# A hybrid SSD, attention and convolution layer: another order of pairs in the input projection, and attention's loads on another queue

## The chip, the cores and the metric

The kernel runs on one core of a Trainium2 chip. A core has a matrix engine (TensorE; PE in the profile, with PEld for its weight loads), three engines for element-wise work (VectorE or DVE, ScalarE or ACT, GpSimd or POOL) and SyncE (SP), which here only issues DMAs. The engines run side by side; each takes its own instructions strictly in order and waits on semaphores for the others. A DMA is issued by an instruction in an engine's queue (SPq, POOLq in the profile) and lands later. The metric is device time in microseconds for one execution; lower is better.

## The reference

One inference step of a one-layer streaming encoder for 1024 prompt positions and 64 positions of a running stream (1088 columns in all). Cut to what matters:

```python
xn = _rmsnorm(x, p['norm_mix_w'])
proj = xn @ p['w_in']
z, xbc, dt_raw, q, k, v, gate_ssm, gate_att = jnp.split(proj, ...)

xbc_c, conv_new = _causal_dwconv(conv_past, xbc, ...)     # 4 taps
xbc_c = jax.nn.silu(xbc_c)                                # then the SSD scan gives y_ssm
y_ssm = _rmsnorm(y_ssm * jax.nn.silu(z))                  # in groups

q = _partial_rope(_rmsnorm(q, p['q_norm_w']), q_pos)
k = _partial_rope(_rmsnorm(k, p['k_norm_w']), q_pos)
s = q @ k.T * ATT_HEAD_DIM ** -0.5                        # two components per head
a = softmax(s)[:, 0] - lam * softmax(s)[:, 1]
o = _rmsnorm(a @ v_all) * (1.0 - lambda_init)

mix = sigmoid(gate_ssm) * (y_ssm @ w_branch_ssm) + sigmoid(gate_att) * (o @ w_branch_attn)
x = x + mix @ w_out
x = x + (silu(conv(rmsnorm(x) @ w_up_a)) * (rmsnorm(x) @ w_up_b)) @ w_down
```

## The kernel before

Every large product is made of three matmuls on split operands: `hi` is the operand rounded to float32r (a cast on ACT, L404), `lo` is the rest (a subtraction on DVE, L405), and the sum is hi x hi + hi x lo + lo x hi. The function `split` (L403) makes both halves.

**Stages in order.** Values and time steps (to about 117 us); the pair stage (117 to 724 us), which projects q, k, z and the convolution's channels; attention over 8 heads (742 to 1120 us), with the gates and the last z tiles as filler between its units; the SSD scan; the branches; the FFN.

**The pair stage.** A pair is two 128-row weight blocks, multiplied by a scheme of 7 block products where a plain one needs 8. Product p takes one combination of the weights (`left[n][p]`, made by `left_parts`, L470 on) and one of the inputs (`parts[PARTS[p], s]`, with `PARTS` = b11, t2, b21, t3, t1, t4, b22). Each product runs in two halves s of 272 columns, with 12 matmuls per half (L553). `in_pair` (L540) is a generator: each `send((p, s))` issues the matmuls of one half and the evacuation behind it. p=0 and p=2 are evacuated by ACT (`u1`, L622; `pre`, L633), the others by DVE with an addition (L624, L626, L635). A pair that has its four quadrants calls `done` (L591): a z pair gets a SiLU on ACT; a q or k pair gets squares (ACT L610, L613; DVE L614) that are summed for its norm; a convolution pair gets, for each of four quadrants, one ACT pass (L581), three DVE passes (L583) and a SiLU (L584). q, k and z pairs are called light here. `INPUT` (L74) gives the order of the 26 pairs: four q, four k, three z, and then three times four convolution pairs and a z pair.

**Where the input parts come from.** b11, b21 and t2 are made in place. t3, t1, t4 and b22 are written to scratch memory p_sc by `rooted` and come back through `load_part` (L534): two loads on SP and a split of each. b12 takes a place that is only free at the stage's end.

**Work beside.** `beside` is a chain of small generators, stepped once in every four sends (L818): `steps` (the time steps' softplus, decays), `cached_keys` (splits of the cached keys), and from pair 3 on `finishing("q")` and `finishing("k")`: for each kind three norm roots (`rstd_of`: ACT Ln L241, Exp L242), twelve row parts (load, scale by DVE L735, split, two stores) and four rotated parts (DVE L749 to L756). Its tiles are called x. The scheduler fixes the order on each engine when the kernel is built; `tc.issue_after(i)` keeps what it encloses behind instruction i.

**Attention.** Per head, `head_tiles` (L883) loads 33 pieces through `load`, which is `nc.sync.dma_start`, SP's queue: q and the halves kh and kl of k for two components c and two column sides x (22 loads; side 0 holds columns 0 to 511), v_t in two loads, and ch_t, cl_t, cv_t of the cache in nine. The side tiles have three buffers, so a component of the next head waits for one of the last. `attend` does one unit: the scores of a block of 128 queries (L959, L960), exponentials (ACT L973), and two units later transposes (L988) and the product with the values (L1008). `ATT_ORDER` = (3, 7, 0, 6, 1, 5, 2, 4, 8): unit i below 8 needs keys up to 128(i+1), unit 8 is the running stream with the cache. Filler comes from `project` (L162), whose weights are loaded by `weights` (L144: load L147 on SP, cast on ACT L148, subtraction on DVE L149). Six such groups (144 matmuls) run between the last pair and the end of the first scores.

Of the kernel before, what the change touches and what calls it, by code (L numbers as in the profile page):

```python
# [9 lines left out]
F32 = mybir.dt.float32  # L10
# [35 lines left out]
B_Q, B_K, B_V, B_Z, B_X, B_G = 0, 8, 16, 20, 36, 60  # L46
WMAX = 4 * (256 + 16)

ATT_ORDER = (3, 7, 0, 6, 1, 5, 2, 4, 8)
BG = 8  # L50
TURNS = ((0, 1), (2,), (3,), (4,), (5,), (6, 7))
# [19 lines left out]


ORDER = (("g", (15, 14)), ("z", range(4 * ZS, 16)), ("g", range(13, 7, -1)), ("g", range(7, 1, -1)))
INPUT = ([(k, i) for k in "qk" for i in range(4)]  # L74
         + [("z", i) for i in range(ZS)] + [x for i in range(ZS) for x in (*(("c", 4 * i + j) for j in range(4)), ("z", ZS + i))])

O_MIX, O_FFN, O_CW, O_CB, O_SN, O_D = 0, 8, 16, 112, 136, 152
O_QN, O_KN, O_FW, O_FB, O_CS = 168, 176, 184, 250, 272
# [5 lines left out]
def hybrid_layer(ctx: ExitStack, tc: tile.TileContext, xT, xt, prm, cst, rope, wvd, win, wbs, wba, wout, wup, wdn,  # L84
# [318 lines left out]
    def split(hi, lo, src):  # L403
        S.copy(hi, src)  # L404
        V.tensor_tensor(out=lo, in0=src, in1=hi, op=ALU.subtract)  # L405

    def cols(s):
        return slice(O2[s], O2[s] + W2[s])
# [108 lines left out]
            left.setdefault(f, {})[x[0]] = x[1]  # L517

    FIRST_BLOCK = dict(q=B_Q, k=B_K, c=B_X, z=B_Z)
    squares, begun_squares = {}, set()  # L520
    seen = {}

# [11 lines left out]
    def load_part(n, at=None):  # L534
        for s in range(2):
            hi, lo = parts[n, s] = units_of(n, s, at)
            load(out=lo.bitcast(F32), in_=p_sc[n].rearrange("(k p) t -> p k t", p=P)[:, :, cols(s)])
            split(hi, lo, lo.bitcast(F32))

    def in_pair(n):  # L540

# [76 lines left out]
        for _ in range(14):  # L618
            p, s = at
            us = cols(s)  # L620
            if p == 0:
                S.copy(u1[:, us], pile("a", p, s, True))  # L622
            elif p == 1:
                seen["read"] = V.tensor_tensor(out=u2[:, us], in0=pile("b", p, s, True), in1=u1[:, us], op=ALU.add)  # L624
            elif p == 3:
                seen["read"] = V.tensor_tensor(out=u1[:, us], in0=pile("b", p, s, False), in1=u1[:, us], op=ALU.add)  # L626
            else:
                r, c, key, start, u = {2: (0, 0, "a", False, None), 4: (1, 1, "c", True, u1), 5: (1, 0, "d", True, u1),
                                       6: (0, 1, "c", False, u2)}[p]
                ps = pile(key, p, s, start)  # L630
                for dst, x in to(r, c, s):
                    if u is None:
                        S.copy(dst, ps[:, x])  # L633
                    else:
                        seen["read"] = V.tensor_tensor(out=dst, in0=ps[:, x], in1=u[:, us][:, x], op=ALU.add)  # L635
                if s == 1:
                    done(r, c)
            at = yield
# [147 lines left out]

    four = row("ss", "st")
    early = [plain_left(0), plain_left(1)]
    for n in ("t3", "t1", "t4", "b22"):
        load_part(n)  # L790
    left = {}
    coming = in_parts(0, early[0])
    for _ in range(7):
# [3 lines left out]
    rest = [(p, s) for p in (1, 3, 4, 5, 6) for s in range(2)]  # L797
    pairs = [begun_in(0), begun_in(1)]
    left[1] = {0: [t[:, :512] for t in early[1]], 2: [t[:, 512:] for t in early[1]]}
    for i in range(2):  # L800
        for at in both:
            pairs[i].send(at)
    for p, s in rest:
        pairs[0].send((p, s))
        if s == 1:
            more_left(1)
    while len(left[1]) < 7:
        more_left(1)
    beside = chain(steps(), cached_keys())
    for n in range(1, len(INPUT)):  # L810
        coming = in_parts(n + 1) if n + 1 < len(INPUT) else iter(())
        u = pairs[1] if n == 1 else begun_in(n)
        for at, (p, s) in enumerate(rest if n == 1 else [(p, s) for p in range(7) for s in range(2)]):
            u.send((p, s))
            if s == 1:
                more_left(n + 1)
            if at % 4 == 0:
                next(beside, None)  # L818
            if n + 1 == len(INPUT) and (p, s) == (1, 1):
                load_part("b12")  # L820
        while n + 1 < len(INPUT) and len(left[n + 1]) < 7:
            more_left(n + 1)
        del left[n]
        if n == 3:
            beside = chain(beside, finishing("q"), finishing("k"))
    run(beside)
    plain = [k_rows(parts, c, s) for c in range(2) for s in range(2)]
# [53 lines left out]
    with (tc.tile_pool(name="ak", bufs=1) as ak, tc.tile_pool(name="at", bufs=1) as at,  # L881
          tc.tile_pool(name="psc", bufs=1, space=PSUM) as psc, tc.tile_pool(name="psa", bufs=1, space=PSUM) as pa):
        def head_tiles(h):  # L883
            def fetch(name, n, b, parts):
                t = ak.tile([P, n], R32, name=name, tag=name, bufs=b)
                for lo, src in parts:
                    load(out=t[lo : lo + src.shape[0]].bitcast(F32), in_=src)
                return t

            by_head = lambda d: [d.rearrange("(x h) t -> h x t", h=16)[2 * h + c] for c in range(2)]  # L890
# [17 lines left out]
            cv_t = ak.tile([P, 4, P], F32, name="cv_t", tag="cv_t", bufs=2)  # L908

            def values_of():  # L910
                load(out=v_t[:, :8], in_=v[0:TP, P * h : P * (h + 1)].rearrange("(a p) e -> p a e", p=P))
                load(out=v_t[:TS, 8], in_=v[TP:T, P * h : P * (h + 1)])

            def cached():
                past(0, ch_t, "ch_t")
                past(1, cl_t, "cl_t")
                load(out=cv_t, in_=cv[:, P * h : P * (h + 1)].rearrange("(a p) e -> p a e", p=P))

            if h == 0:
                for x in range(2):  # L920
# [154 lines left out]
        for h in range(8):  # L1075
# [7 lines left out]
            s0 = at.tile([P, 9], F32, name="s0", tag="s0", bufs=2)  # L1083
            V.memset(ssq, 1.0)
            V.memset(s0, 1.0)
            for x, i in enumerate(ATT_ORDER):
                unit = attend(h, i, tiles, o_t, ssq, s0)
                next(unit)
                next(ended, None)
                done = None  # L1090
                if i == ATT_ORDER[-1]:
                    done = lambda h=h, o=o_t, q=ssq, s=s0: head_out(h, o, q, s)
                waiting.append((unit, done))
                settle(DEEP, ATT_STEPS)
# [708 lines left out]
```

## Time and profile before

| | |
|---|---|
| Median of three runs | 2511.06 us (2508.02 to 2512.3) |
| The profiled execution, its own time | 2511.3 us |
| Span of its instructions | 2509.5 us |
| Matmul clock granted, mean | 0.991 |
| DMA, share of 16 engines | 52.5% SP's queue, 3.4% POOL's |

The page gives busy time per engine and what ended the idle time ahead of a group of instructions. A view by stretches gives busy time for each engine between two moments. The timeline lists instructions by start, with a bracket that says how long the engine had been idle and which instruction released it. L numbers are lines of this kernel; a matmul's duration overlaps with the next one's, so a group's share is better read from busy time than from the mean. DMA rows give the count, the size of each and the median time from issue to landing.

### The profile page before, as it was taken

The page shows a single profiled execution, that of the slowest core. Times are in us where ns is not written, and L with a number is a line of the kernel's source. Part 1 is how long each engine was busy: PE and PEld are TensorE (multiplying, and loading weights), DVE is VectorE, ACT ScalarE, POOL GpSimd, SP SyncE. Part 2 cuts the span into 40 slices and gives each one's busy share as a digit, 9 for nine tenths or more (in the row PEclk, how much of TensorE's full clock was granted, in tenths as well). Part 3 has the DMA queues.
Part 4 walks back from the last instruction along what each step waited for, and adds up shares of the span by engine and source line. Part 5 has one row for each costly group of instructions (what it writes and reads, how often), then busy time and mean ns, then how long its engine had stood idle before and what let it go on. Part 6 is the DMA issues. An engine that isn't in the chain of part 4 may idle for free.

```text
span 2509.5 us, 48443 instructions
## 1 busy us (share of the span) xinstructions
PE 2390.5 (95%) x18504; PEld 2302.9 (92%) x18504; DVE 1782.3 (71%) x3063; ACT 1231.0 (49%) x2615; POOL 720.0 (29%) x702
## 2 busy tenths in 40 slices
PE   8999999989989899999999999999999999999999
PEld 8999998888988788889888899999999999999999
DVE  4595778889957776762778765665977777776763
ACT  7344446435435566554767664434443333343441
POOL 0012213344400000000534342002264554544433
PEclk9999999999999999999999999999999999999999
DMA  7845463754265565525598973766123335258874
GB/s 252 271 154 190 176 225 109 247 186 145 100 185 167 158 184 154 161 90 199 192 333 274 309 253 128 216 183 208 56 88 144 114 113 185 78 208 224 221 204 83
DMA packets 282442, 449.72 MB, mean 179 GB/s; under 512 B 34969, under 2 KB 185634, under 8 KB 282210
## 3 DMA queue, kind: packets, MB, share of 16 engines
q1 hardware_dynamic: 275010, 433.54, 52.5%
q0 software_dynamic: 7200, 13.09, 3.4%
q8 instruction: 145, 2.38, 0.4%
q14 instruction: 87, 0.71, 0.1%
HBM read 294.03 MB, written 152.50 MB: 178 GB/s over the span
## 4 chain that ended last, share of the span: by engine, by line
PE 62%; DVE 13%; DMA 11%; ACT 6%; issue 4%; POOL 2%; SPq 1%; DVEq 0%; POOLq 0%; ACTq 0%
PE mx L553 9%; PE mx L1464 8%; PE mx L1622 5%; PE mm L155 5%; PE mm L157 5%; PE mm L156 5%; PE mm L553 4%; PE mm L1464 3%; PE mx L155 2%; PE po L1008 2%; PE mm L1622 2%; PE mx L157 2%; PE mx L156 2%; DMA ht<-h_sc 2%; DVE cc L583 1%
## 5 line engine op out<-in xcount | busy, mean ns | idle before, releaser
L155 PE MATMUL mm<-b,w_hi 128*128 128x272 f32 x1152 | 342.9, 298 | 4.8 <-ACT w_hi L148 2.9
L157 PE MATMUL mm<-b,w_lo 128*128 128x272 f32 x1152 | 339.5, 295 | 2.1 <-DVE w_lo L149 2.1
L156 PE MATMUL mm<-b,w_hi 128*128 128x272 f32 x1152 | 340.1, 295 | 0.0
L155 PEld LDWEIGHTS mm<-b,w_hi 128*128 128x128 f32 x1152 | 220.3, 191 | 9.8 <-issue 3.7
L157 PEld LDWEIGHTS mm<-b,w_lo 128*128 128x128 f32 x1152 | 219.8, 191 | 5.8 <-DVE w_lo L149 3.7
L156 PEld LDWEIGHTS mm<-b,w_hi 128*128 128x128 f32 x1152 | 220.3, 191 | 3.0 <-issue 2.1
L1143 POOL TENSOR_SCALAR_AFFINE_SELECT bc<-bc 128x1024 f32<-128x1024 f32 (+1 forms) x36 | 43.0, 1196 | 581.6 <-DMA start<-in_st_dram 471.7
L480 POOL TENSOR_TENSOR ws<-w_f 128x512 f32<-128x512 f32 (+1 forms) x56 | 79.5, 1420 | 416.4 <-DVE ss L614 159.9
L405 DVE TENSOR_TENSOR wh<-w_f,wh 128x512 fp32r<-128x512 f32 (+1 forms) x174 | 163.3, 939 | 46.5 <-ACT wh L404 46.1
L404 ACT CAST w_hi<-ws 128x512 fp32r<-128x512 f32 (+1 forms) x120 | 73.3, 611 | 186.0 <-PE mx L1464 84.6
L1464 PE MATMUL mx<-n,wh 128*128 128x272 f32 x1128 | 150.1, 288 | 1.9 <-ACT wh L404 1.3
L1464 PE MATMUL mx<-m,w_hi 128*128 128x272 f32 x752 | 146.0, 291 | 3.1 <-DVE hb L1500 2.9
L1464 PEld LDWEIGHTS mx<-n,wh 128*128 128x128 f32 x1128 | 144.5, 188 | 2.5 <-ACT wh L404 1.6
L973 ACT ACTIVATE p_t<-sc,mx 128x512 f32<-128x512 f32 (+5 forms) x144 | 106.1, 739 | 66.3 <-DVE mx L964 22.8
L583 DVE SCALAR_TENSOR_TENSOR cc<-pre,par,cc 128x544 f32<-128x544 f32 (+1 forms) x144 | 131.9, 937 | 0.3 <-ACT cc L581 0.2
L404 ACT CAST wh<-w_f 128x512 fp32r<-128x512 f32 (+1 forms) x174 | 106.5, 615 | 50.1 <-issue 15.3
L553 PE MATMUL mx<-t,wh 128*128 128x272 f32 x840 | 116.0, 291 | 11.6 <-DVE u L624 10.3
L1464 PEld LDWEIGHTS mx<-m,w_hi 128*128 128x128 f32 x752 | 119.0, 190 | 4.2 <-DVE hb L1500 3.8
L553 PE MATMUL mx<-t,w_hi 128*128 128x272 f32 x608 | 118.5, 291 | 3.6 <-DVE pre L635 3.6
L553 PEld LDWEIGHTS mx<-t,wh 128*128 128x128 f32 x840 | 109.5, 189 | 13.5 <-DVE u L624 11.6
L1481 POOL TENSOR_TENSOR hb<-hb,cc 128x544 f32<-128x544 f32 (+2 forms) x66 | 88.0, 1346 | 113.1 <-DVE hb L1502 56.2
L553 PE MATMUL mx<-b,wh 128*128 128x272 f32 x840 | 115.6, 290 | 2.3 <-ACT u L622 1.7
(447 smaller groups left out, 7373.3 us busy)
## 6 DMA issues: line engine op xcount, KB each, us to landing
w_f<-in_win_dram SPq DMA_DIRECT2D x78, 512.0 KB, 3.9
w_f<-in_wup_dram SPq DMA_DIRECT2D x45, 512.0 KB, 3.7
bc<-a_sc SPq DMA_DIRECT2D x32, 512.0 KB, 6.1
h_sc<-hb SPq DMA_DIRECT2D x44, 272.0 KB, 2.1
ht<-h_sc SPq DMA_DIRECT2D x22, 544.0 KB, 5.4
t_sc<-ht SPq DMA_DIRECT2D x22, 544.0 KB, 3.1
out_dram<-yq POOLq DMA_DIRECT2D x44, 272.0 KB, 5.5
g_sc<-gt SPq DMA_DIRECT2D x64, 136.0 KB, 2.5
```

What stands on the lines that cost most here:

```text
L155: PE.matmul(ps, a_hi, b_hi, start=i == 0, stop=False)
L156: PE.matmul(ps, a_hi, b_lo, start=False, stop=False)
L157: PE.matmul(ps, a_lo, b_hi, start=False, stop=i == n - 1)
L404: S.copy(hi, src)
L405: V.tensor_tensor(out=lo, in0=src, in1=hi, op=ALU.subtract)
L480: by.tensor_tensor(out=s1, in0=q21, in1=q22, op=ALU.add)
L553: seen["mm"] = PE.matmul(ps, w[x][:, c], b[y][:, k], start=start and k == i == 0, stop=k == 3 and i == 2, skip_group_check=not start)
L583: V.scalar_tensor_tensor(cc[:, :n], pre[:, i : i + n], cw(i), cc[:, :n], ALU.mult, ALU.add)
L973: act(p_t[:n, :nk], sc[c][:n, :nk], AF.Exp, bias=mx[:n, c : c + 1], accum_out=dst)
L1464: PE.matmul(ps, w[x][:, c], b[y][:, k], start=start and k == i == 0, stop=k == 3 and i == 2, skip_group_check=not start)
L1481: G.tensor_tensor(out=hb[h][:, o : o + n], in0=hb[h][:, o : o + n], in1=cc[:, d : d + n], op=ALU.mult)
L1622: PE.matmul(ps, w[y][:, c], b[z][:, k], start=start and k == j == 0, stop=k == n - 1 and j == 2, skip_group_check=not start)
```

## The change

Four edits. The line numbers behind L72 move by a few lines.

1. `INPUT`: a light pair and a convolution pair in turn, for twelve rounds, with z pairs 4 and 5 at the end. The generators `finishing` join `beside` behind pair 7 (`Q_DONE`), where the last q pair and the fourth convolution pair are done, and not behind pair 3.
2. `load_part` only loads. t1, t4 and b22 are asked for behind t3's second load. The splits are a function of their own, `split_part`, called in the order in which the products need them, each kept behind an evacuation: t3 behind pair 0's first four sends, t1 behind pair 1's, t4 behind p=1 and b22 behind p=3 of pair 0, b12 likewise near the end.
3. All 33 loads of a head go through `G.dma_start`, POOL's queue.
4. Head 0 takes its units as (3, 0, 2, 1, 7, 5, 6, 4, 8): the first four need only side 0. The other heads keep `ATT_ORDER`.

```diff
+ATT_FIRST = (3, 0, 2, 1, 7, 5, 6, 4, 8)
 ATT_ORDER = (3, 7, 0, 6, 1, 5, 2, 4, 8)
...
-INPUT = ([(k, i) for k in "qk" for i in range(4)]
-         + [("z", i) for i in range(ZS)] + [x for i in range(ZS) for x in (*(("c", 4 * i + j) for j in range(4)), ("z", ZS + i))])
+LIGHT = [(k, i) for k in "qk" for i in range(4)] + [("z", i) for i in range(2 * ZS)]
+INPUT = [x for i in range(12) for x in (LIGHT[i], ("c", i))] + LIGHT[12:]
+Q_DONE = 7
...
     FIRST_BLOCK = dict(q=B_Q, k=B_K, c=B_X, z=B_Z)
+    LATER = {1: "t4", 3: "b22"}
...
     def load_part(n, at=None):
         for s in range(2):
             hi, lo = parts[n, s] = units_of(n, s, at)
-            load(out=lo.bitcast(F32), in_=p_sc[n].rearrange("(k p) t -> p k t", p=P)[:, :, cols(s)])
-            split(hi, lo, lo.bitcast(F32))
+            seen["part"] = load(out=lo.bitcast(F32), in_=p_sc[n].rearrange("(k p) t -> p k t", p=P)[:, :, cols(s)])
+
+    def split_part(n, *behind):
+        with ExitStack() as pins:
+            for x in behind:
+                pins.enter_context(tc.issue_after(x.ins))
+            for s in range(2):
+                hi, lo = parts[n, s]
+                split(hi, lo, lo.bitcast(F32))
...
             if p == 0:
-                S.copy(u1[:, us], pile("a", p, s, True))
+                seen["copy"] = S.copy(u1[:, us], pile("a", p, s, True))
...
                     if u is None:
-                        S.copy(dst, ps[:, x])
+                        seen["copy"] = S.copy(dst, ps[:, x])
...
     early = [plain_left(0), plain_left(1)]
-    for n in ("t3", "t1", "t4", "b22"):
-        load_part(n)
+    load_part("t3")
+    for n in ("t1", "t4", "b22"):
+        with tc.issue_after(seen["part"].ins):
+            load_part(n)
...
-    for i in range(2):
+    for i, x in enumerate(("t3", "t1")):
         for at in both:
             pairs[i].send(at)
+        split_part(x, seen["copy"])
     for p, s in rest:
         pairs[0].send((p, s))
         if s == 1:
             more_left(1)
+            if p in LATER:
+                split_part(LATER[p], seen["copy"], seen["read"])
...
             if n + 1 == len(INPUT) and (p, s) == (1, 1):
                 load_part("b12")
+                split_part("b12", seen["copy"], seen["read"])
...
-        if n == 3:
+        if n == Q_DONE:
             beside = chain(beside, finishing("q"), finishing("k"))
...
             def fetch(name, n, b, parts):
                 t = ak.tile([P, n], R32, name=name, tag=name, bufs=b)
                 for lo, src in parts:
-                    load(out=t[lo : lo + src.shape[0]].bitcast(F32), in_=src)
+                    G.dma_start(out=t[lo : lo + src.shape[0]].bitcast(F32), in_=src)
                 return t
...
             def values_of():
-                load(out=v_t[:, :8], in_=v[0:TP, P * h : P * (h + 1)].rearrange("(a p) e -> p a e", p=P))
-                load(out=v_t[:TS, 8], in_=v[TP:T, P * h : P * (h + 1)])
+                G.dma_start(out=v_t[:, :8], in_=v[0:TP, P * h : P * (h + 1)].rearrange("(a p) e -> p a e", p=P))
+                G.dma_start(out=v_t[:TS, 8], in_=v[TP:T, P * h : P * (h + 1)])
...
-                load(out=cv_t, in_=cv[:, P * h : P * (h + 1)].rearrange("(a p) e -> p a e", p=P))
+                G.dma_start(out=cv_t, in_=cv[:, P * h : P * (h + 1)].rearrange("(a p) e -> p a e", p=P))
...
-            for x, i in enumerate(ATT_ORDER):
+            for x, i in enumerate(ATT_ORDER if h else ATT_FIRST):
...
-                if i == ATT_ORDER[-1]:
+                if x == 8:
                     done = lambda h=h, o=o_t, q=ssq, s=s0: head_out(h, o, q, s)
```

## The prediction

> **What bounds the kernel now.** I read the page first, then busy time by stretches, then the timeline around each long stall of TensorE.
>
> ```profile
> span 2509.5 us, 48443 instructions
> PE 2390.5 (95%) x18504; PEld 2302.9 (92%) x18504; DVE 1782.3 (71%) x3063; ACT 1231.0 (49%) x2615; POOL 720.0 (29%) x702
> ```
>
> TensorE is busy 95% of the span, and the change removes no matmul. So a gain can only come out of PE's 119 us of idle time and out of stretches at half clock. The stretches below say where they lie; columns are length, then busy time and instructions of PE, PEld, DVE, ACT, POOL, then granted clock, DMA share, GB/s.
>
> ```profile
> 117.40:723.50 606.10, 569.69 (x4406) 560.47 (x4405) 493.19 (x801) 291.50 (x519) 190.85 (x216) 0.99 0.51 170
> 117.40:282.80 165.40, 159.10 (x1222) 156.19 (x1221) 118.00 (x201) 75.15 (x141) 32.94 (x24) 0.98 0.52 172
> 282.80:394.10 111.30, 107.08 (x846) 106.41 (x845) 84.31 (x140) 48.06 (x91) 30.44 (x29) 1.00 0.62 212
> 394.10:601.20 207.10, 181.89 (x1381) 176.58 (x1381) 184.42 (x295) 107.44 (x184) 79.73 (x100) 0.99 0.53 177
> 641.60:705.40 63.80, 63.80 (x506) 63.69 (x506) 62.02 (x94) 32.41 (x58) 31.45 (x42) 1.00 0.30 103
> 742.00:1120.00 378.00, 339.59 (x2447) 309.85 (x2446) 265.10 (x655) 220.13 (x640) 0.00 (x0) 0.98 0.52 156
> ```
>
> The first row is the pair stage, with 606.1 - 569.7 = 36.4 us of PE idle. A pair is 168 matmuls (7 products, 2 halves, 12 each); the fifth row holds 506/168 = 3.0 pairs, so a pair costs PE 63.8/3 = 21.2 us. That row is three convolution pairs with nothing beside them: DVE 62.0/3 = 20.7 us per pair, and PE never waits. The third row is mostly light pairs, with the q finishing beside them: 4.2 us idle over 5.0 pairs, DVE at 84.3 of 107.1 us of PE work. The fourth is mostly convolution pairs with the k finishing beside them: 25.2 us idle, DVE busy 184.4 us against 181.9 us of PE. There DVE carries more than PE has work to cover.
>
> ```profile
> PE mx L553 <- DVE u L624: 10.3, 6, 3.3
> PE mx L553 <- DVE pre L635: 9.3, 8, 2.9
> PE mx L553 <- ACT u L622: 6.7, 2, 4.9
> ```
>
> PE's waits inside the stage say the same: they are for evacuations that stand late in DVE's order, and 4.9 us of the third row is one wait at the stage's start.
>
> **The change part by part.**
>
> *Loads and splits of the last operands, in order of use.* The stage's start, before:
>
> ```profile
> 123.29 0.29 PE L553 MATMUL mx<-b,w_lo 128*128 128x272 f32 x1
> 128.52 0.59 PE L553 MATMUL mx<-b,w_hi 128*128 128x272 f32 x1 [4.95 <-ACT u L622]
> ...
> 124.04 1.10 ACT L404 CAST b<-b 128x1088 fp32r<-128x1088 f32 x1 [5.34 <-DMA b<-p_b]
> 127.09 1.10 ACT L404 CAST t<-t 128x1088 fp32r<-128x1088 f32 x1 [0.41 <-DMA t<-p_t]
> 128.09 1.24 ACT L622 COPY u<-mx 128x272 f32<-128x272 f32 x4
> ...
> 127.20:134.00 6.80, 5.48 (x24) 5.48 (x25) 5.95 (x7) 5.48 (x10) 0.00 (x0) 0.50 1.04 322
> ```
>
> ACT holds casts of b22 and t3, which wait for their DMAs, ahead of the four u1 copies (x4) that PE needs. The stall is 4.95 us, and the last row shows what follows it: 6.8 us at a granted clock of 0.50, about 6.8/2 = 3.4 us more. In the changed order the four copies stand first on ACT, the t3 splits come after them, and t3's two loads go first on SP. PE then has eight groups of 12 matmuls plus p=1's two groups before it needs t3: from 117.4, ten groups of 21.2/14 = 1.5 us, to about 132.5. First loads landed by 124; two casts of 1.10 and two DVE subtractions of about 1.3 us end well before 132.5. t1, t4 and b22 follow at one product (3 us) each, against 2.2 us of casts for each. Taken: the whole 8.3 us; bounds 4 (a late t4 or b22 still stops PE for as long as the stall itself) and 8.3.
>
> *Light and convolution pairs in turn; finishing from pair 8 on.* Instruction counts on PE, DVE and ACT stay the same but for table loads; only order changes. The finishing's DVE work, counted by its tile x over the stage:
>
> ```profile
> 117.40:723.50 606.10, 88.52 (x112) 25.59 (x40) 0.99 0.51 170
> ```
>
> 88.5 us, of which the cached keys are a small part, over 52 steps of a quarter pair: some 6.5 us per pair over 13 pairs. Before, the k half lay on convolution pairs: 20.7 + 6.5 = 27.2 us of DVE against 21.2 of PE. After, steps run in pairs 1 to 5, and finishing in pairs 8 to 20, which are 6 convolution and 7 light pairs. What is left for a light pair is (493.2 - 12 x 20.7 - 88.5)/14 = 11.2 us, steps and first splits still in it, so 9.5 is nearer. Sum: 6 x 20.7 + 7 x 9.5 + 85 = 276 us of DVE, against 13 x 21.2 = 276 of PE. So the overload goes, but without reserve. At 79% DVE load (third stretch) the lumps of finishing still cost 4.2/5.0 = 0.84 us per pair. Taken for these 13 pairs: 13 x 0.84 = 11, plus 6 for the first of them (four k pairs with their squares are heavier), 17 us.
>
> The first eight pairs now hold four convolution pairs. Before, the second stretch had 118.0 us of DVE in 159.1/21.2 = 7.5 light pairs, steps, keys, first splits and some two pairs' worth of q finishing (13) included. So 118 - 13 + 5 for the missing half pair + 4 x (20.7 - 9.5) = 155 of 170 us; idle 2 us. The last five are light enough for none.
>
> The table switches grow. Before:
>
> ```profile
> L241 ACT ACT_TABLE_LOAD x3 | 3.8, 1283 | 0.4 <-DVE ss L245 0.4
> L242 ACT ACT_TABLE_LOAD x3 | 3.8, 1283 | 3.2 <-DMA q_st<-x 3.2
> L584 ACT ACT_TABLE_LOAD x3 | 3.8, 1283 | 0.1
> ```
>
> Only the k roots sat between SiLUs. In the changed order the q roots do too, and so do two of the steps: 10 more loads of 1.283 us in the stage, 12.8 us of ACT. ACT is busy 291 of 606 us, so this is hidden except where a u1 copy queues behind it: 3 us taken. If that cover is gone, 12.8. Middle of the stage after: 17 + 2 + 3 = 22 us idle, against 36.4 - 4.95 = 31.4 before: a gain of 9.5 us. Bounds: 0 (all idle stays) and 31.
>
> *Heads' loads on POOL's queue, other first units.* The start of attention, before:
>
> ```profile
> 739.20 0.59 SPq L911 DMA_DIRECT2D v_t<-out_dram  x1
> 741.09 0.94 SPq L147 DMA_DIRECT2D w_f<-in_win_dram  x2
> 749.15 1.04 ACT L148 CAST w_hi<-w_f 128x1024 fp32r<-128x1024 f32 x1 [6.59 <-DMA w_f<-in_win_dram]
> 751.60 0.80 PE L959 MATMUL sc<-kh,q 128*128 128x512 f32 x1 [8.13 <-ACT p_t L973]
> 748.40:755.20 6.80, 3.41 (x11) 2.87 (x12) 3.05 (x6) 3.49 (x7) 0.00 (x0) 0.50 0.68 198
> ```
>
> The gate's weights stood on SP behind head 0's 24 loads; ACT's cast waited for them ahead of the first exponentials, and PE waited 8.13 us, then ran 6.8 us at half clock: 8.1 + 3.4 = 11.5 us. After, SP carries none of the 264 head loads (33 per head) and asks for these weights ahead of the first gate store. What is late next is the head itself. POOL's pace and the landing times:
>
> ```profile
> 2422.60 1.75 POOL L1607 DMA_DIRECT2D out_dram<-yq  x2 [3.73 <-DVE yq L1641]
> 2360.85 2.67 POOL L1607 DMA_DIRECT2D out_dram<-yq  x3 [3.36 <-DVE yq L1641]
> kh<-k_st SPq DMA_DIRECT2D x32, 144.0 KB, 3.6
> v_t<-out_dram SPq DMA_DIRECT2D x8, 512.0 KB, 4.2
> 783.83 1.24 SPq L887 DMA_DIRECT2D kl<-k_st  x2
> ```
>
> Back to back POOL issues one DMA in 0.88 us, SP one in 0.62. In the changed order the first load waits for p=5 of the last pair, one product (3 us) before the stage's end E. Units 3, 0, 2, 1 need only the first 11 loads: issued by E+7, landed by E+11; the second component's scores come after 120 filler matmuls, E+15. Unit 7 needs loads 12 to 22, landed by E+20, wanted at about E+25. v_t is load 23 and has eight times as many pieces per row, so its issue costs between 0.88 and 8 x 0.88 = 7 us: landed between E+22 and E+28, wanted at E+25. Hence 1.5 us lost of the 11.5, 10 us gained; bounds 4 and 11.5.
>
> At each later head 15 loads follow the release of the first buffer:
>
> ```profile
> 777.65 1.08 SPq L887 DMA_DIRECT2D kh<-k_st  x2
> 793.52 0.47 PE L959 MATMUL sc<-kh,q 128*128 128x512 f32 x1
> ```
>
> 15 x 0.88 + 3.6 = 16.8 us after 777.65, so 794.5 against 793.5; in the changed order 48 more filler matmuls (6 us) stand ahead of that score. Taken as nothing. POOL computes nothing in these 378 us (sixth stretch), so no work of its own queues behind a waiting load; a head takes 378/8 = 47.2 us and its loads 33 x 0.88 = 29.
>
> **The sum.** The profiled execution took 2511.3 us (span 2509.5 and 1.8 around it), 0.2 above the median of 2511.06. 2511.3 - 8.3 - 9.5 - 10 = 2483.5; I say 2483.
>
> **The rivals.**
>
> *DVE stays the limit.* Pairs 8 to 20 have DVE at 276 of 276 us and more table loads; if idle stays 31 us there, only the two starts gain: 2511.3 - 18.3 = 2493. For it: the fourth stretch, DVE at 89% of the time and still 25 us lost. Against: the fifth, 97% and nothing lost. Chance 0.20.
>
> *The first stalls only change their name.* A late t4 and b22, and v_t at 7 us of issue: 4 + 4 us from the starts, nothing in the middle, 2503. It is the case that the change doesn't do what it says. Chance 0.08.
>
> *POOL's queue becomes the bound of attention: slower.* One mechanism: issue on POOL takes longer beside DVE. It decides from 47.2/33 = 1.43 us per load; at 1.6 us a head takes 52.8, eight heads 45 us more, and with 18 us gained earlier 2538. For it: the order within a head leaves under 2 us to spare at 0.88. Against:
>
> ```profile
> L964 DVE TENSOR_REDUCE mx<-sc 128x1 f32<-128x1024 f32 x16 | 19.5, 1219 | 0.2
> L995 DVE COPY a_t<-pt 128x512 f32<-128x512 f32 x23 | 15.7, 681 | 7.2 <-PE pt L988 7.0
> ```
>
> DVE moves 1024 elements in 1219 ns and 512 in 681, under one per ns; no faster mode shows, and POOL kept 0.88 beside a working DVE. Chance 0.12.
>
> The Trainium skill, SBUF — State Buffer, "SBUF: two separate sides", speaks for this rival: while VectorE runs in a mode that takes both port pairs, GpSimd cannot write the descriptors of its DMAs, and the page advises the other queues. By that rule, if such a mode ran in attention, the time would be this rival's 2538 and not 2483; the two rows above show none, so the trace leaves the rule without its condition.
>
> **How the numbers follow.** Forecast 0.60, the rivals 0.20, 0.08 and 0.12. The forecast's own range is 2466 (middle idle 5 us) to 2493. The range 2464 to 2508 takes in the first two rivals and leaves out the slower one and the unlikely end, where all idle goes (2511.3 - 36.4 - 5 - 11.5 = 2458). About 0.2%, 5 us, can be told from no change here: faster 0.80 (forecast, first rival, most of the second, less a little of the forecast's tail), same 0.06, slower 0.14.
>
> **What would show it.** Right: no wait of PE over 1 us for u L632 near 123, no half clock there; the pair stage near 588 us with no stretch as bad as the fourth; no wait near 8 us at the first scores; POOL's load issues near 0.9 us. Wrong: waits for DVE's evacuations still above 25 us in pairs 8 to 20; PE waits on kh, kl or v_t at each head's start; issue spacing on POOL above 1.4 us.

## The result, and the profile after

The changed kernel is slower. Its median is 2519.86 us (20 runs, 2514.38 to 2527.18) against 2512.2 us for the kernel before (20 runs, 2499.61 to 2523.55). The ratio is 1.0034, with a 95% interval of 1.0021 to 1.0047. The forecast was 2483 us.

The page of the changed kernel; its profiled execution took 2515.76 us:

```profile
span 2513.9 us, 48469 instructions
PE 2399.4 (95%) x18504; PEld 2311.0 (92%) x18504; DVE 1794.6 (71%) x3063; ACT 1246.9 (50%) x2625; POOL 872.0 (35%) x966
```

The instruction counts are the announced ones: 10 more on ACT (table loads) and 264 more on POOL (the heads' loads). DVE has the same 3063 instructions as before, yet is busy 12.3 us longer.

Both kernels by stretches, cut at the first matmul of pairs 0, 2, 11 and 21, at the end of the pair stage, and at the last head's transposes (columns: length; busy time and instructions of PE, PEld, DVE, ACT, POOL; granted clock; DMA share; GB/s). Before:

```profile
117.40:169.30 51.90, 45.60 (x339) 44.73 (x337) 40.87 (x63) 24.42 (x43) 5.43 (x4) 0.93 0.54 174
169.30:369.20 199.90, 196.73 (x1541) 194.24 (x1542) 140.79 (x240) 88.41 (x168) 50.92 (x37) 1.00 0.56 191
369.20:617.20 248.00, 221.06 (x1688) 215.32 (x1687) 221.07 (x358) 126.75 (x217) 93.96 (x120) 0.99 0.53 175
617.20:723.50 106.30, 106.30 (x844) 106.19 (x843) 90.47 (x144) 51.92 (x91) 40.54 (x55) 1.00 0.35 119
723.50:1151.80 428.30, 389.89 (x2844) 359.02 (x2843) 275.53 (x686) 236.26 (x681) 0.00 (x0) 0.98 0.51 156
1151.80:2509.50 1357.70, 1320.51 (x10394) 1274.36 (x10393) 949.47 (x1436) 639.35 (x1264) 528.91 (x482) 0.99 0.59 184
```

After:

```profile
116.80:168.20 51.40, 44.64 (x338) 43.54 (x337) 43.47 (x66) 26.17 (x44) 6.60 (x9) 0.96 0.52 170
168.20:368.40 200.20, 198.51 (x1543) 195.45 (x1542) 166.69 (x270) 109.43 (x187) 73.54 (x82) 0.99 0.42 148
368.40:614.90 246.50, 225.59 (x1688) 219.78 (x1687) 211.54 (x335) 119.86 (x211) 82.82 (x89) 0.97 0.58 197
614.90:728.00 113.10, 108.44 (x844) 107.73 (x843) 80.76 (x131) 48.41 (x88) 35.43 (x41) 0.98 0.43 140
728.00:1157.70 429.70, 394.85 (x2846) 364.01 (x2845) 277.31 (x686) 238.72 (x681) 140.74 (x260) 0.97 0.53 155
1157.70:2513.90 1356.20, 1318.27 (x10394) 1273.02 (x10392) 950.36 (x1435) 640.39 (x1264) 532.69 (x482) 0.99 0.59 184
```

Pairs 0 and 1 gain 0.5 us (forecast: 8.3). Pairs 2 to 25 take 200.20 + 246.50 + 113.10 = 559.8 us against 554.2: they lose 5.6 (forecast: a gain of 9.5). Attention loses 1.4 (forecast: a gain of 10). The load did move: 25.9 us of DVE's work went into pairs 2 to 10, which still have only 1.7 us of idle time. Pairs 11 to 20 have 9.5 us less of it, and PE's idle time there fell from 26.9 to 20.9 us; but PE is busy 4.5 us longer with the same 1688 matmuls, so only 1.5 us are left. And pairs 21 to 25, where PE never waited before, take 6.8 us more. The spans of the two profiled executions differ by 4.4 us, the medians by 7.7.

**The clock.** Part of every difference here is the granted clock: for short spells PE runs at half clock. Two pairs of neighbouring stretches of the kernel before, each 3.41 us long, show how it goes:

```profile
553.82:557.23 3.41, 0.83 (x6) 0.83 (x7) 3.16 (x5) 1.68 (x3) 2.42 (x4) 1.00 0.83 245
557.23:560.64 3.41, 3.41 (x17) 3.41 (x16) 3.41 (x5) 0.84 (x1) 1.55 (x1) 0.50 0.10 37
...
874.68:878.09 3.41, 1.62 (x13) 1.45 (x14) 3.41 (x8) 1.33 (x4) 0.00 (x0) 1.00 0.79 258
878.09:881.50 3.41, 3.41 (x28) 3.03 (x27) 2.61 (x7) 2.29 (x9) 0.00 (x0) 1.00 0.84 261
```

All half-clock spells of one execution lie on one grid of 3.41 us. The window after one with 2.58 us of PE idle time runs at 0.50 (17 matmuls); the one after 1.79 us of idle time runs at full clock (28 matmuls). Counted over all twenty profiled executions from 30 us on, for windows that follow one at full clock: with less than 1.5 us idle none of 13790 is followed by half clock, with 1.5 to 2.0 us 64 of 203 are, with 2.0 us or more 224 of 224. Behind a window that is itself at half clock less is enough: with 0.75 us or more idle in it the next is at half clock too in 63 of 63 cases, with less than 0.5 us in 1 of 270. A window at half clock costs a busy PE 1.7 us. So a wait of 2 to 3 us costs nothing on top, 1.7 us or 3.4, as the grid cuts it and as other waits follow. The Trainium skill, TensorE: Matmul & The Clock Gate, "HAM oscillation — how this bites in real kernels", gives the rule as no idle gaps above some 3.4 us; these rows don't agree, 2 us in one window are enough. That the window is free-running, which the same page of the Trainium skill says under "What's actually happening", agrees with the rows of the twenty executions: the grid lies differently in each.

The share of the clock that was not granted, times the span, gives the time lost to it. The profiled execution of before lost (1 - 0.991) x 2509.5 = 22.6 us; over 142 further runs of the same kernel, made beside the experiments, the mean is 28.9. The 20 runs of the changed kernel lost 33.1. So the clock carries some 4 us of the difference, as far as runs that were not made side by side can show it, and the profile from which the forecast was made was a lucky one by 6.

### The profile page after: what moved, and what is told of

It reads as the page before. It is cut to its first block, busy times and chain, and to the rows that moved or that the text cites. A ratio compares the mean times of both kernels' runs of the same rounds, so it can differ in the third digit from the quotient of the medians.

```text
span 2513.9 us, 48469 instructions
## 1 busy us (share of the span) xinstructions
PE 2399.4 (95%) x18504; PEld 2311.0 (92%) x18504; DVE 1794.6 (71%) x3063; ACT 1246.9 (50%) x2625; POOL 872.0 (35%) x966
## 4 chain that ended last, share of the span: by engine, by line
PE 56%; DVE 16%; DMA 13%; issue 6%; ACT 6%; POOL 2%; SPq 1%; POOLq 0%; DVEq 0%; ACTq 0%
PE mx L1480 10%; PE mx L563 6%; PE mm L157 5%; PE mm L159 5%; PE mm L158 5%; PE mm L1480 4%; PE mx L1638 3%; PE po L1024 2%; PE mm L563 2%; DVE cc L593 2%; PE mm L1638 2%; DVE wh L407 1%; PE mx L157 1%; PE mx L159 1%; PE mx L158 1%
## 5 line engine op out<-in xcount | busy, mean ns | idle before, releaser
L407 DVE TENSOR_TENSOR wh<-w_f,wh 128x512 fp32r<-128x512 f32 (+1 forms) x174 | 167.8, 965 | 48.7 <-ACT wh L406 48.3
L989 ACT ACTIVATE p_t<-sc,mx 128x512 f32<-128x512 f32 (+6 forms) x144 | 106.1, 740 | 70.8 <-DVE mx L980 25.3
L563 PEld LDWEIGHTS mx<-b,wh 128*128 128x128 f32 x840 | 111.1, 192 | 6.8 <-DVE wh L407 3.9
```

The costliest lines, as they stand in the source:

```text
L563: seen["mm"] = PE.matmul(ps, w[x][:, c], b[y][:, k], start=start and k == i == 0, stop=k == 3 and i == 2, skip_group_check=not start)
L989: act(p_t[:n, :nk], sc[c][:n, :nk], AF.Exp, bias=mx[:n, c : c + 1], accum_out=dst)
```

## The experiments

Each kernel was timed in five rounds beside the kernel before; the ratios are against that. Those of the first four:

| | edit | ratio | 95% interval |
|---|---|---|---|
| e1 | before, with the loads and splits in order of use | 1.0021 | 1.0008 to 1.0033 |
| e2 | before, with the turn of pairs | 1.0040 | 1.0025 to 1.0055 |
| e3 | before, with the heads' loads on POOL | 1.0016 | 1.0002 to 1.0030 |
| e4 | changed kernel without the turn | 1.0014 | 1.0002 to 1.0026 |

**One edit at a time.** e1:

```diff
-            split(hi, lo, lo.bitcast(F32))
...
+    def split_part(n, *behind):
...
+            if p in LATER:
+                split_part(LATER[p], seen["copy"], seen["read"])
```

> The kernel before with one edit: the last operands' loads and splits in order of use. Theory A (the turn of light and convolution pairs is what costs): the 4.95 us wait near 128 and the half clock behind it go, as in the changed kernel, and nothing comes back at 148 to 170, since no convolution pair stands there: 5 to 8 us faster than before (about 2505 us), PE busy at least 48.5 us in 150:200. Theory B (the edit only moves the stall): the waits that the changed kernel shows at 148 to 166 (5.6 us, and 6.8 us at half clock behind them) are those of the late splits and come here too: within 3 us of before.

Theory B's mechanism, not its time. The waits of PE over 0.4 us in pairs 0 to 2, from the timeline of e1 (start, duration, instruction; in the bracket the idle time and what ended it):

```profile
124.28 0.52 PE L561 MATMUL mx<-b,w_hi 128*128 128x272 f32 x2 [1.53 <-ACT u L630]
...
148.55 0.39 PE L561 MATMUL mm<-t,w_lo 128*128 128x272 f32 x1 [1.05 <-DVE w_lo L405]
...
162.81 1.77 PE L561 MATMUL mx<-b,wh 128*128 128x272 f32 x12 [1.67 <-DVE u L634]
...
179.44 0.75 PE L679 MATMUL st<-st,con 128*128 128x288 f32 x2 [1.79 <-DVE nacum L675]
```

The 4.95 us are 1.53 now, and 1.05 + 1.67 + 1.79 us stand behind them: 6.0 us in all, where before had 4.95 and 1.12. Only the half clock went, since each piece is under 2 us. The median is 2517.85 us, 4.4 above before and outside B's 3 us; nothing in the trace of pairs 0 to 2 explains that.

e2:

```diff
-INPUT = ([(k, i) for k in "qk" for i in range(4)]
-         + [("z", i) for i in range(ZS)] + ...)
+INPUT = [x for i in range(12) for x in (LIGHT[i], ("c", i))] + LIGHT[12:]
...
-        if n == 3:
+        if n == Q_DONE:
```

> The kernel before with one edit: light and convolution pairs in turn, finishing from pair 8 on. Theory A: waits in the middle stay near 30 us in sum but are many, each with its 3.4 us of half clock; the pair stage gets 5 to 9 us longer than the 606.1 of before and the time is 2517 to 2521 us. Theory C (the heads' loads on the POOL queue are what costs, the turn is neutral): within 3 us of before, the pair stage 603 to 609 us.

Theory A, just above its range: 2521.74 us, pair stage 116.70 to 729.70 = 613.0 us. Over its runs the clock cost 34.0 us, 6.4 more than in the runs of before beside it.

e3 (the four `load(` of attention's fetches become `G.dma_start(`):

> The kernel before with one edit: the heads' loads on the POOL queue. Theory A: the 8.13 us wait at the first scores goes or shrinks, but its 11.5 us come back in part at later units: 0 to 6 us faster (2506 to 2512 us). Theory C: each head's 15 loads behind the release come later than on SP, heads 1 to 7 lose about 1.5 us each, and the time is 4 us or more above before.

2519.05 us, 0.16% slower, so theory A's gain isn't there. But C's reason isn't either: heads 1 to 7 have 26.5 us of PE idle time, 27.2 before. The 8.13 us wait is now one of 2.60 behind ACT's first gate evacuation, one of 1.65 and one of 5.34.

e4 (the old `INPUT` and `if n == 3` in the changed kernel):

> The changed kernel with the old order of pairs and finishing from pair 3 on; the other three edits stay. Theory A: 2500 to 2506 us, faster than before by 6 to 12 us. Theory C: about 2518 us, slower than before.

2517.46 us: a miss by more than 10 us for A, and C's number. Taking the turn out wins 1.0034/1.0014, 0.2%, and what is left is still not faster than before. Each edit alone came out slower, by 0.16 to 0.40%. Only the turn's loss is well clear of what the kernel before shows against itself (e17 below: off by 0.07%, with an interval that reaches 0.20% from 1). The three don't add up either: 0.77% in sum, 0.34% together.

**Where finishing stands.** e5 and e11 change the changed kernel, e6 and e7 the kernel before:

```diff
+FIN_AT = (0, 2, 5, 7, 10, 12)
...
-            if at % 4 == 0:
+            if at % 4 == 0 if n <= Q_DONE else INPUT[n][0] != "c" and at in FIN_AT:
```

(`Q_DONE` is 3 for e6 and e7, and `FIN_AT` is (4, 5, 7, 8, 10, 11) for e11.)

> The changed kernel, but finishing is stepped in light pairs alone, six steps in each, and in no convolution pair. Theory L (the waits of the middle come from lumps: a finishing step stands on DVE next to a convolution pair's nine passes, ahead of the evacuation that PE waits for; DVE's mean load is not the cause): TensorE's idle time in pairs 8 to 25, 25.7 us in the changed kernel, falls below 12, the half clock in the stage with it, and the time is 2500 to 2508 us. Theory M (DVE's load over the stage is what binds, wherever the steps stand): idle time stays above 20 us there and the time is 2516 to 2522 us.

> The kernel before with one edit: finishing is stepped in light pairs alone, six steps in each (pairs 4 to 10, then the three single z pairs). Theory L: the 26.9 us of idle time in pairs 11 to 20 fall to what the three single z pairs' steps leave, under 10 us, and the time is 2494 to 2502 us. Theory M: light pairs with six steps have 19.7 us of DVE in 21.2, so the waits move to pairs 4 to 10, 15 us or more of idle there, and the time is within 4 us of before.

> The kernel before with two edits: the last operands' loads and splits in order of use, and finishing in light pairs alone. If the loads' edit costs by itself, as its run alone was 4 us above before, this is 3 to 5 us slower than the kernel with light finishing alone; if that was chance of the half-clock windows, it is equal or up to 3 us faster.

> The changed kernel with finishing stepped in light pairs alone, and there only from the first half of product 2 (send 4) to that of product 5's second half (send 11), so that no step stands between a convolution pair's last nine passes and the next pair's addition for product 1. Theory T (that place is what is late in the changed kernel, 13.1 us of waits at the first half of product 3): those waits fall below 5 us and the time is 2503 to 2510 us. Rival R: the idle time of pairs 8 to 25 stays above 20 us, and the time is 2510 us or more, as with six steps spread over the whole light pair (2512).

e5: ratio 0.9993 (0.9979 to 1.0008), 2511.98 us, but with 24.2 us idle in pairs 8 to 25, so L's reason fails: of the 10 us that the ratios give it over the changed kernel, 7 are clock (26.2 us lost instead of 33.1). e6: 1.0021 (1.0007 to 1.0036); the waits moved to pairs 5 to 10 (17.4 us there, 3.2 before), as M said. e7: 1.0013 (0.9998 to 1.0028), no slower than e6, so the loads' edit isn't worse by itself on that base. e11: 1.0011 (0.9997 to 1.0025), 8.2 us still at the first half of product 3, 27.0 us idle in pairs 8 to 25; rival R. In these four kernels PE is idle 32 to 35 us in the pair stage, in the changed one 34.0.

**Which product waits.** In all these kernels most waits of the middle stand ahead of product 3 or product 6. Product 3 goes on in product 1's PSUM bank, so it needs DVE to have read that; product 6 likewise product 4's. e9, e10 and e12 give product 3 a bank of its own:

```diff
-                ... in0=pile("b", p, s, False), in1=u1[:, us], op=ALU.add)
+                ... in0=pile("e", p, s, True), in1=u2[:, us], op=ALU.add)
```

> The kernel before with one edit: product 3 writes a PSUM bank of its own and is added to u2, where it went on in the bank of product 1 and was added to u1 (u2 is that bank plus u1, so the sum is the same). Theory S (TensorE's waits in the middle are for that bank: product 3 may not begin before DVE has read product 1 out of it, and DVE does that late): the 17.1 us of waits at the first and second half of product 3 in pairs 2 to 25 fall below 4 us, the pair stage gets 10 us or more shorter and the time is 2496 to 2505 us. Rival R (DVE as a whole is late, and PE stops at the next place that needs it): idle time in pairs 2 to 25 stays above 24 us of 30.9, and the time is within 3 us of before.

> The changed kernel with product 3 in a bank of its own. Theory S: the 17.2 us at product 3 fall below 4, the half clock behind these waits goes too, and the time is 2500 to 2508 us, 12 us or more under the changed kernel's. Rival R: 2516 to 2522 us.

> The kernel before with two edits: head 0 begins with units 3, 0, 2, 1, and product 3 has a bank of its own. If the two gains are apart, theory S gives 2491 to 2501 us, faster than both kernels; by rival R it is the 2509 us of the first units alone.

The waits of PE in pairs 11 to 20 of e9 (in us: total, times, longest):

```profile
PE mx L553 <- DVE pre L635: 14.8, 7, 3.3
PE mm L553 <- DVE pre L635: 4.8, 2, 2.4
PE mx L553 <- ACT u L622: 3.6, 2, 2.4
```

No wait for `u` of DVE is left, which were 10.3 + 3.2 us; the same time stands behind `pre`, at product 6. Ratio 1.0000 (0.9986 to 1.0013). In e10 product 3 has under 1 us and product 6 has 29; 1.0040 (1.0023 to 1.0058). e12: 1.0001 (0.9991 to 1.0011). Rival R in all three (e10, at 2524.99 us, even above its range): a dependency taken away gives nothing, since DVE is late for whatever comes next. Its own waits say why. DVE in pairs 11 to 20 of the kernel before:

```profile
DVE x L735 <- DMA x<-k_r: 10.6, 6, 3.2
DVE wh L405 <- ACT wh L404: 5.8, 5, 3.2
...
DVE u L624 <- PE mx L553: 0.4, 1, 0.4
```

and of the changed kernel:

```profile
DVE x L745 <- DMA x<-k_r: 9.7, 8, 3.3
DVE cc L593 <- ACT cc L591: 4.6, 3, 3.0
DVE x L759 <- DMA x<-k_r: 4.1, 1, 4.1
DVE x L745 <- DMA x<-q_r: 3.6, 4, 2.0
...
DVE pre L645 <- PE mx L563: 1.7, 3, 0.8
```

DVE waits for PE 0.4 us in 248.0 and 1.7 in 246.5. So its queue sets the pace of this stretch in both kernels: before, 221.1 us busy and 26.4 of waits for DMAs and ACT at the head of its queue; after, 211.5 busy and 32.9 of such waits. Of the 9.5 us of work that the change took away there, 6.5 came back as waits.

DVE's work is not all of that limit. The chain of work that ended last, followed back through pairs 11 to 20, lies on PE for 10% of the time before and 9% after; on DVE for 43% and 36%; on DMAs for 23% and 33%. Finishing's loads of x and its stores alone are 17% and 29%: x shares two buffers (`fx`, L61), so a load starts only when the store of an earlier x has landed.

**Taking finishing off DVE.** e13 (on before) and e14 (on the changed kernel):

```diff
-            split(hi, lo, x)
+            S.copy(hi, x)
+            G.tensor_tensor(out=lo, in0=x, in1=hi, op=ALU.subtract)
...
-                V.scalar_tensor_tensor(x, x, wcol(j), rs[:, c : c + HT], ALU.mult, ALU.mult)
+                G.tensor_tensor(out=x, in0=x, in1=rs[:, c : c + HT], op=ALU.mult)
+                act(x, x, AF.Identity, scale=wcol(j))
```

> The kernel before with finishing's element-wise work (88 us of DVE with the cached keys, and the waits for x in front of it) on POOL, and its scale by the norm's weight on ACT. Theory D (DVE is the bound of pairs 11 to 20 by its work plus its own waits at the head of its queue): TensorE's idle time in pairs 2 to 25 falls from 30.9 to below 10 us, and the time is 2490 to 2503 us. Rival P (POOL beside DVE slows DVE's operations by as much): DVE's three convolution passes take over 1.03 us each (0.937 before) and the time is 2510 us or more.

> The changed kernel with finishing's element-wise work on POOL. Theory D: idle time in pairs 2 to 25 from 26.2 to below 10 us, time 2495 to 2506 us; the turn then costs nothing, since the load that it was to spread is gone. Rival P: 2515 us or more.

Rival P, and worse: 1.0093 (1.0075 to 1.0111) and 1.0107 (1.0090 to 1.0125), with 40.4 and 45.6 us idle in pairs 2 to 25. Two groups of DVE over pairs 11 to 20 (busy time, then mean ns of one); before:

```profile
L583 DVE SCALAR_TENSOR_TENSOR cc<-pre,par,cc 128x544 f32<-128x544 f32 x48 | 46.2, 973 | 0.0
...
L635 DVE TENSOR_TENSOR pre<-mx,u 128x272 f32<-128x272 f32 x31 | 13.1, 432 | 0.0
```

e13:

```profile
L583 DVE SCALAR_TENSOR_TENSOR cc<-pre,par,cc 128x544 f32<-128x544 f32 x48 | 53.8, 1128 | 20.0 <-ACT cc L581 12.1 <-issue 4.2 <-POOL x L736 3.5
...
L635 DVE TENSOR_TENSOR pre<-mx,u 128x272 f32<-128x272 f32 x30 | 12.4, 429 | 0.2
```

With POOL busy beside it, the convolution pass, whose operands both lie in SBUF, takes 16% longer; the evacuation from PSUM takes no longer. The Trainium skill, SBUF — State Buffer, "SBUF: two separate sides", says that a VectorE operation with two SBUF inputs and a GpSimd operation that reads SBUF shut each other out; these rows agree. Even before, the pass has two speeds (in ns: shortest, median, longest):

```profile
L583 DVE SCALAR_TENSOR_TENSOR cc<-pre,par,cc x144: 767/778/1827, 385.1 to 708.8; 128x544 f32<-128x544 f32 x72, 128x547 f32<-128x547 f32 x72
```

With no POOL instruction beside it, the 128x544 form takes 776 ns on average in the kernel before (42 of 72) and 777 in e13 (31); with POOL at work all along, 1138 (20) and 1199 (25). POOL's work in the stage is mostly the weights' combinations (`ws`, `w_f`, L480 to L509). An estimate, each form of DVE's operations priced at its median with POOL idle: POOL's work costs DVE 61 of its 493 us in the pair stage before, 75 of 502 in the changed kernel, and 30 of 221 and 35 of 212 in pairs 11 to 20. The 14 us more cover the 9.2 us by which DVE is longer busy in the changed stage. No run here takes POOL's work away.

ACT, which in e13 stands 17.7 us for POOL ahead of x's scale and 13.6 ahead of the convolution's first pass, made DVE wait 42 us in pairs 11 to 20. So these two runs set a new limit; that DVE's queue is the old one rests on the rows of the section before, not on them.

**Steps spaced evenly.** e15 (on before) and e16 (on the changed kernel) step the work beside the pairs at every fourth send counted through.

```diff
-            if at % 4 == 0:
+            sends += 1
+            if sends % 4 == 0:
```

> The kernel before with the steps beside the pairs at every fourth send counted through, 6.1 us apart, where they were 6.1, 6.1, 6.1 and 3.0 us apart; the work stays on DVE. If the waits for x count by themselves: DVE's waits for the loads of x in pairs 11 to 20 fall from 13 to below 6 us, PE's idle time in pairs 2 to 25 by about as much, and the time is 2504 to 2511 us. If only the work counts: within 3 us of before.

> The changed kernel with evenly spaced steps. If the waits for x count by themselves: DVE's waits for loads in pairs 11 to 20 fall from 19 to below 8 us, and the time is 2508 to 2515 us. If only the work counts: 2517 to 2522 us.

0.9995 (0.9985 to 1.0005) and 1.0016 (1.0003 to 1.0028). DVE's waits for DMAs in pairs 11 to 20 fell from 15.4 to 11.6 us in e15 and from 19.1 to 18.3 in e16, not by half, and its waits for ACT rose from 10.8 to 20.1 and from 13.6 to 22.5. So the edit didn't do what it was for, and whether the waits for x count by themselves stays open. Loading x earlier, with a third buffer, was not tried.

**The first units, and the floor.** The floor is what the kernel before shows against itself. e8 and e18 are the kernel before with `ATT_FIRST`; e17 is the kernel before itself.

> The kernel before with one edit: head 0 begins with units 3, 0, 2, 1. The gates' weights still stand on SP behind head 0's loads. If the first units alone carry the 2.6 us of idle time that the changed kernel saves in head 0, this is 2 to 4 us faster than before; if they need the loads on POOL's queue, the 8.13 us wait stays and the time is within 2 us of before.

> The kernel before, unchanged, as if it were an edit. If the comparison is sound to 0.1%, the ratio is 0.999 to 1.001 and its interval holds 1. In its profile the rule read from the other runs (a window of 3.41 us runs at half clock after one in which TensorE stood idle for more than about 1.8 us) picks other waits than in the first profile, and the untouched part after attention takes some us more or less than the 1357.7 of the first.

> The kernel before with head 0 beginning with units 3, 0, 2, 1, once more. If the 0.17% of the first comparison is an effect, the ratio is again below 0.9995 (2508 to 2512 us); if it was chance, it is within 0.1% of 1.

e8: 0.9983 (0.9967 to 0.9998); e18: 0.9991 (0.9978 to 1.0004); e17: 0.9993 (0.9980 to 1.0005). The first units alone can't be told from the kernel run against itself, and no version here is shown to beat the kernel before. The wait at the first scores stays in e8:

```profile
746.91 0.69 PE L960 MATMUL sc<-kh,q 128*128 128x384 f32 x1 [7.88 <-ACT p_t L974]
```

The second profile of the kernel before, pair stage and attention:

```profile
117.20:722.30 605.10, 575.48 (x4406) 566.73 (x4405) 494.11 (x800) 290.87 (x519) 190.52 (x216) 0.98 0.51 170
722.30:1156.70 434.40, 397.28 (x2846) 365.83 (x2844) 275.69 (x686) 236.56 (x681) 0.00 (x0) 0.96 0.51 153
```

Its stage is as long as in the first profile, but with 29.6 us of idle time, where the first has 36.4, and PE 5.8 us longer busy at a lower clock; its first wait is 3.01 us, not 4.95; its attention is 6.1 us longer with no more idle time. Five profiles have the pair stage of before (before, e3, e8, e17, e18): 603 to 608 us, mean 606, with 29.6 to 36.4 us idle, mean 33.6. The two with the turn and finishing as the change has it (after, e2) have 611.2 and 613.0 us, with 34.0 and 37.1 idle. One profile of this kernel doesn't carry terms of a few us.

## Why the prediction was wrong

*Start of the stage, 8.3 us.* Mis-sized, and the mechanism was half right. The wait for ACT's copy near 123 shrank to 0.89 us, as forecast. But the forecast priced the splits by their durations and asked only whether each landed before its product. It didn't follow what they push back: in the changed kernel most of the stall stands 20 to 40 us later,

```profile
PE mx L563 <- DVE wh L407: 3.6, 1, 3.6
PE mx L563 <- ACT u L632: 1.7, 2, 0.9
PE mm L563 <- DVE w_lo L407: 1.1, 1, 1.1
```

(waits of PE in pairs 0 and 1), where DVE is to split pair 1's and 2's weights; and 3.64 of it is long enough for 6.8 us at half clock again. The second rival, the stall that only changes its name, came nearest, though it blamed a late t4 and b22 and not the weights. The 3.64 us need two edits together: e1 and e4, with the old order of pairs, have 1.67 and 1.85 us at that place, and e2, the turn alone, has no wait there; pair 1 is a convolution pair only with the turn. With the old order the edit does gain a little at the start: pairs 0 and 1 take 47.9 us in e1 and 48.3 in e4, against 48.9 to 51.9 in five profiles without it. The stall itself was also one execution's: 4.95 us there, 3.01 in e17.

*Middle, 9.5 us.* The terms held, and what was left out beside them cost more than the gain. For pairs 8 to 20 the forecast set 276 us of DVE against 276 of PE and took 17 us of waits and 3 for the table loads. That stretch after, whole:

```profile
302.50:614.90 312.40, 291.42 (x2198) 284.58 (x2197) 271.05 (x425) 162.76 (x281) 108.51 (x114) 0.98 0.54 187
```

271 us of DVE and 312.4 - 291.4 = 21.0 us of idle time: both terms held. The steps that failed stand beside them.

First, "the last five are light enough for none": pairs 21 to 25 have 4.7 us of idle time and one window of half clock. Finishing's rotated parts reach into pair 21, a convolution pair, and the waits there are 2.87 us at product 6 and 1.11 at the next pair's product 3. Pairs 21 to 25 take 106.2 to 106.3 us in five profiles with the old order and finishing as before, and 113.1 and 114.0 in the two with the new.

Second, PE is busy 291.4 us in 13 pairs that need 276 where nothing waits. The sum had half clock only behind the two starts; here it costs 6.8 us, four windows, and most of the rest was there before as well (285.2 us busy with 1.7 lost to the clock, 291.7 with 10.2 in e17). Eight waits over 1.9 us lie in the changed kernel's stage, each a candidate for a window.

Third, the 31.4 us from which the gain was taken were one execution's, and 1.3 of them lay in pairs 0 and 1: pairs 8 to 20 had 30.1 us of idle time there and 24.2 in e17. So in idle time the changed kernel wins 3 to 9 us in pairs 8 to 20 against these two profiles of before, and gives 4.7 back behind them. Over more profiles less is left: in pairs 2 to 25, the five of before and the two with the new order (after, e2) have 28.2 and 30.2 us of idle time on average, lose 6.5 and 9.9 us to the clock, and take 555.7 and 562.2 us.

The first rival's reason, DVE as the limit, holds for pairs 11 to 20 of both kernels, with x's loads and stores as a part of it, though its 31 us of idle time did not stay: 21.0 did. It fits that no other place of the steps and no other bank made a kernel faster than before; "without reserve" had counted DVE's work and not its 26.4 us of own waits. The ten table loads are on ACT; PE's waits for ACT in pairs 11 to 20 are 1.4 us after and 2.6 before, so no price of their own shows.

*Start of attention, 10 us.* Mis-sized; the mechanism was incomplete. POOL was faster than feared: back to back, loads leave at 0.52 to 0.55 us each, and v_t's large one takes 0.94 where the forecast had 0.88 to 7. But its queue also stops for landings: head 0's first 22 loads take 17.5 us. And a load lands later than from SP's queue, kh's larger ones after 4.7 us in the median instead of 3.6. The 8.13 us wait is gone. What came instead, from the timeline of the changed kernel:

```profile
725.31 0.75 POOL L903 DMA_DIRECT2D q<-q_st  x1 [27.00 <-PE mx L563]
...
729.56 0.32 SPq L625 DMA_DIRECT2D z_sc<-pre  x1
...
737.33 0.40 ACT L859 ACTIVATE gt<-mm 128x272 f32<-128x272 f32 x1 [7.80 <-DMA z_sc<-pre]
...
737.78 0.59 PE L157 MATMUL mm<-b,w_hi 128*128 128x272 f32 x1 [2.87 <-ACT gt L859]
...
800.42 2.45 DVE L1042 SCALAR_TENSOR_TENSOR o_t<-o_t,ors,wsub 128x128 f32<-128x128 f32 x9
...
806.24 0.79 PE L975 MATMUL sc<-kh,q 128*128 128x512 f32 x1 [3.92 <-ACT p_t L989]
```

The last z pair's store leaves when eight or more of POOL's loads are already on their way, and lands 7.7 us later; the first gate evacuation waits for it. At 806 head 1's scores wait while DVE works through the nine scalings of head 0's end, 2.45 us that stand ahead of the reductions for these scores. Both waits are over 2 us, and 6.8 us of half clock follow each. Head 0's idle time, from the first score to its transposes, fell from 11.2 to 8.6 us: 2.6 gained of the 10, and the clock took that back (11.9 us lost to it in the attention stretch, 6.8 before).

*POOL as the bound of attention.* The rival fell by its own point: 0.52 us per load against 1.43. The heads after the first have 26.2 us of idle time, 27.2 before; "taken as nothing" was right.

So the sign was missed because all three gains were waits taken at the length of one execution, with no later consumer and no new half clock put behind them. In the profiles the start gains 0.5 us, the middle loses 5.6 and attention 1.4. What stays open: why the loads' edit alone and the heads' loads alone come out slower than before, if by more than the floor; and what DVE's longer operations cost in time, since no run takes POOL away from beside them.

## What to carry to other kernels

A wait that is removed is worth what the next one in line leaves of it; follow the pushed-back work to its own consumer before counting the gain. Whether an in-order engine has reserve is told by whether it ever waits for its producer in that stretch, not by its busy share: count its waits for loads and for other engines into its load, and ask what slows its operations. And take a second profile before summing terms of a few microseconds.

## What the runs showed of the hardware

A window of half clock follows one of 3.41 us at full clock with 2.0 us or more of idle time in 224 of 224 cases, on a grid that lies differently in each execution, so the same kernel lost 22.6 us to it in one profile and (1 - 0.984) x 2516.4 = 40 us in the other. POOL issues plain loads at 0.52 us each back to back, and stops for landings. A convolution pass of DVE, with two operands in SBUF, takes 776 ns with POOL idle and 1138 with POOL at work beside it; an addition out of PSUM takes 435 and 430.
